# A decoder layer of two feed-forward steps, sparse attention and a pooling mixer on one core: gate and up of the first step by Strassen's seven products, and the mixers placed ahead in the program

## The chip, the core and the metric

The kernel runs on one core of one Trainium2 chip. The metric is device time in microseconds (us), the median of three runs. Five engines have their own instruction streams: PE (TensorE, the matrix products), DVE (VectorE), ACT (ScalarE), POOL (GpSimd) and SP (SyncE, which here only issues transfers). PEld is the loading of a stationary operand, which overlaps PE. PEclk is the granted TensorE clock as a share of its upper level.

## The reference

1024 tokens of width 1024 go through one layer, all in float32.

```
x = x + 0.5 * swiglu(rms_norm(x, ffn1_norm), ffn1_w_gate, ffn1_w_up, ffn1_w_down)   # inner width 2816
h = rms_norm(x, mix_norm)
q, k, v, qi, ki, wi, u = split(h @ w_in, (512, 512, 512, 256, 64, 4, 512))
q, k: RMS norm per head (8 heads x 64), rotary; qi (4 heads x 64), ki: rotary
I[t, s] = sum_h wi[t, h] * relu(qi[t, h] . ki[s])          # indexer, causal
attn = softmax over the 256 keys of highest I per query    # 8 heads
pooled = trailing means (2, 4, 8, 16) of u minus u, a 128x128 map per group, a scale
x = x + concat(attn, pooled) @ w_out
x = x + 0.5 * swiglu(rms_norm(x, ffn2_norm), ffn2_w_gate, ffn2_w_up, ffn2_w_down)
swiglu(x, g, u, d) = (silu(x @ g) * (x @ u)) @ d
```

## The kernel before

**Precision and units of work.** Each float32 operand is written as a high and a low part, and each product is three matrix multiplications (high by high, high by low, low by high; `mm3`, line 62). A full matmul has a 128x128 stationary operand and 512 moving columns. Weights come from DRAM as they are, 256 KB at a time, and are split on the chip by `weight`: ACT copies the high part (L171), DVE or POOL subtracts to get the low one (L172). Where `alone` is set DVE takes all of these, else POOL takes two of three.

**Halves.** The tokens are worked on in two halves of 512. A half's normalised and transposed activations live in the SBUF region XA (half 0) or XB (half 1). `ffn(h, ...)` goes over the 22 blocks of 128 inner columns: gate, up, silu times up (L200 to L204), and after each four blocks a down product that is added to x (L220). `mixer(h, ...)` holds index projection, indexer scores, pooling mixer, projections of v, k and q, top-k masks, attention and output projection. Its top-k (`top_masks`) finds each query's 256th highest score bit by bit in 31 steps; a step is an exclusive-or (L444), a count of one tile of 128 queries on ACT (L445) and of one on DVE (L429), a comparison (L450) and a conditional copy (L451), each waiting for the one ahead. `attention` goes over 4 head pairs, 2 query pairs and 2 heads, 16 turns; a turn has logits (L510, L511), softmax (L512 to L519), transposes (L533), splits (L537, L538) and value products (L541, tile `pv`), one turn behind the logits. Queries, keys, values and the mixer's output go through DRAM (`q_dr`, `k_dr`, `v_dr`, `m_dr`); the loads back are issued by POOL (L243, L488, L489, L497).

**What sets the order.** The kernel emits the work in the order of its last lines; a scheduler then orders each engine's instructions by what is ready in its model, earlier emitted work first, and by the free buffers of each tile pool (`BUFS`, `PBUFS`: 3 banks `fg` for the feed-forward steps; 2 `ba`, 2 `bt` and 1 `pv` for the mixers). Each engine runs its stream in that order. The emission is: x of half 0; the first step on half 0 (4 blocks); x of half 1, its norm; the rest of the first step on half 0; mixer 0 and the second norm of half 0; the whole first step on half 1; mixer 1 and the second norm of half 1; the second step on half 0, then on half 1. So `ffn(1, hT1, w1)`, 1584 full matmuls, stands beside mixer 0, and the second step of half 0 beside mixer 1, as what TensorE can do while a mixer waits; it is called filler below.

Of the kernel before, what the change touches and what calls it, by code (L numbers as in the profile page):

```python
# [18 lines left out]
S = 1024  # L19
# [13 lines left out]
HIGH = 10_000_000  # L33


@with_exitstack
def hybrid_layer(ctx: ExitStack, tc: tile.TileContext, x, ffn1_norm, ffn1_w_gate, ffn1_w_up,
# [7 lines left out]
    BUFS = {"r": 3, "w": 6, "a": 4, "t": 2, "br": 3, "bw": 3, "sc": 4, "mk": 4, "qm": 2,  # L45
            "st": 4, "cs": 1, "sel": 2, "x8": 4}
    PBUFS = {"fg": 3, "ba": 2, "bt": 2, "pv": 1}
    uid = [0]

    def t(tag, shape, dt=F32):  # L50
        uid[0] += 1
        return sb.tile(shape, dt, name=f"{tag}{uid[0]}", tag=tag, bufs=BUFS.get(tag, 1))
# [4 lines left out]

# [598 lines left out]
```

## Time and profile before

| what | value |
|---|---|
| median of 3 runs | 1988.79 us (1988.09 to 1989.29) |
| profiled execution, span from first to last instruction | 1985.0 us |
| PE busy in that span | 1936.2 us (98%) |
| DVE, ACT, POOL busy | 1115.9, 835.3, 555.2 us |
| mean granted TensorE clock | 0.995 |
| moved by DMA | 241.59 MB, mean 122 GB/s |

The span is that of one profiled execution; the median of the unprofiled runs is 3.8 us above it, which stands for what lies around the span. A share of busy time is an average over stages, and says nothing of what a stage waits for; that is read from windows of the trace.

### The profile page before, as it was taken

What the parts mean: (1) busy time and instruction counts of PE and PEld (TensorE: products, weight loads), DVE (VectorE), ACT (ScalarE), POOL (GpSimd) and SP (SyncE); (2) the same over time, 40 slices, a digit from 0 to 9 for tenths busy, and PEclk for the clock granted to TensorE, in tenths of its full rate; (3) what the DMA queues carried; (4) which work ended last, traced back from release to release, by engine and by line L of the source; (5) the groups of instructions that cost most, each with busy time, mean ns of one, the idle gap of its engine ahead of it and who ended that gap; (6) DMA issues with size and microseconds to landing.
All of it is one profiled execution on the core that took longest, in us unless ns stands there. A gap on an engine that the chain in (4) does not pass through costs nothing.

```text
span 1985.0 us, 25600 instructions
## 1 busy us (share of the span) xinstructions
PE 1936.2 (98%) x8904; PEld 1592.5 (80%) x8904; DVE 1115.9 (56%) x2242; ACT 835.3 (42%) x1550; POOL 555.2 (28%) x550
## 2 busy tenths in 40 slices
PE   7999999999999999999999998999999999999999
PEld 6888888888778888888888777678888878888887
DVE  5434433535985686242447999966767433444344
ACT  5323223344443566232443565437575332322231
POOL 2000000134448643344443343774332210000000
PEclk9999999999999999999999999999999999999999
DMA  7223323434365666333453225485653613333232
GB/s 210 88 89 101 96 90 97 137 110 128 100 167 154 174 157 198 130 91 97 135 137 97 78 93 149 136 199 128 131 140 113 201 42 96 102 95 96 91 106 90
DMA packets 304273, 241.59 MB, mean 122 GB/s; under 512 B 35472, under 2 KB 254736, under 8 KB 304144
## 3 DMA queue, kind: packets, MB, share of 16 engines
q1 hardware_dynamic: 285520, 207.45, 35.2%
q0 software_dynamic: 18624, 32.51, 7.6%
q8 instruction: 70, 1.15, 0.2%
q14 instruction: 59, 0.48, 0.1%
HBM read 208.45 MB, written 31.46 MB: 121 GB/s over the span
## 4 chain that ended last, share of the span: by engine, by line
PE 79%; DVE 13%; issue 3%; POOL 1%; ACT 1%; DMA 1%; SPq 0%; DVEq 0%; POOLq 0%; ACTq 0%
PE fg L62 63%; PE ba L62 6%; PE bt L62 5%; DVE x L429 4%; PE pv L62 2%; PE bt L533 2%; DVE sel L451 1%; DVE sel L450 1%; DVE sel L444 1%; DVE w L172 1%; DVE x L220 1%; POOL st L134 1%; PE ba L150 1%; DMA r<-in_ffn_w_gate_dram 0%; DVE sel L448 0%
## 5 line engine op out<-in xcount | busy, mean ns | idle before, releaser
L171 ACT CAST w<-r 128x512 fp32r<-128x512 f32 x528 | 325.5, 619 | 588.7 <-PE fg L62 304.0
L62 PE MATMUL fg<-XA,w 128*128 128x512 f32 x2112 | 519.6, 398 | 0.2
L62 PE MATMUL fg<-w,a 128*128 128x512 f32 x2112 | 505.4, 393 | 3.5 <-DVE x L220 2.3
L62 PE MATMUL fg<-XB,w 128*128 128x512 f32 x2112 | 497.5, 392 | 0.1
L62 PEld LDWEIGHTS fg<-XA,w 128*128 128x128 f32 x2112 | 394.8, 189 | 90.4 <-ACT XA L153 0.5
L62 PEld LDWEIGHTS fg<-w,a 128*128 128x128 f32 x2112 | 394.0, 188 | 87.5 <-DVE x L220 4.8
L62 PEld LDWEIGHTS fg<-XB,w 128*128 128x128 f32 x2112 | 395.4, 189 | 82.0 <-ACT XB L153 0.5
L172 DVE TENSOR_TENSOR w<-r,w 128x512 fp32r<-128x512 f32 x352 | 255.1, 727 | 317.0 <-ACT w L171 315.2
L172 POOL TENSOR_TENSOR w<-r,w 128x512 fp32r<-128x512 f32 x176 | 234.2, 1335 | 709.2 <-ACT w L171 357.0
L220 DVE SCALAR_TENSOR_TENSOR x<-fg,x 128x512 f32<-128x512 f32 x192 | 129.9, 686 | 122.0 <-PE fg L62 121.6
L172 POOL TENSOR_TENSOR bw<-br,bw 128x512 fp32r<-128x512 f32 (+1 forms) x75 | 95.1, 1273 | 154.8 <-ACT bw L171 146.8
L201 DVE TENSOR_TENSOR t<-t,fg 128x512 f32<-128x512 f32 x88 | 60.2, 684 | 106.4 <-PE fg L62 102.5
L171 ACT CAST bw<-br 128x512 fp32r<-128x512 f32 (+1 forms) x112 | 65.9, 596 | 119.9 <-PE bt L62 101.0
L200 ACT ACTIVATE t<-fg 128x512 f32<-128x512 f32 x88 | 52.4, 596 | 98.1 <-PE fg L62 97.7
L62 PE MATMUL ba<-bw,XB 128*128 128x512 f32 (+1 forms) x288 | 74.7, 384 | 7.1 <-DVE bw L172 2.7
L62 PE MATMUL ba<-bw,XA 128*128 128x512 f32 (+1 forms) x288 | 75.4, 386 | 2.1 <-ACT bw L171 2.1
L172 DVE TENSOR_TENSOR bw<-br,bw 128x512 fp32r<-128x512 f32 (+1 forms) x37 | 27.2, 736 | 86.8 <-ACT bw L171 86.4
L62 PE MATMUL bt<-bw,XB 128*128 128x512 f32 (+1 forms) x288 | 73.5, 382 | 1.6 <-ACT sc L365 1.3
L62 PE MATMUL bt<-bw,XA 128*128 128x512 f32 (+1 forms) x288 | 73.4, 382 | 0.2 <-DVE sel L448 0.2
L445 ACT ACTIVATE x<-sc,sel 128x384 bf16<-128x384 f32 (+1 forms) x62 | 44.6, 719 | 58.9 <-DVE sel L444 57.7
L204 POOL TENSOR_TENSOR a<-t,a 128x512 fp32r<-128x512 f32 x44 | 59.3, 1348 | 35.0 <-ACT a L203 34.6
L62 PEld LDWEIGHTS ba<-bw,XB 128*128 128x128 f32 x288 | 52.1, 189 | 20.2 <-DVE bw L172 3.9
(179 smaller groups left out, 1964.5 us busy)
## 6 DMA issues: line engine op xcount, KB each, us to landing
r<-in_ffn_w_gate_dram SPq DMA_DIRECT2D x176, 256.0 KB, 3.1
r<-in_ffn_w_up_dram SPq DMA_DIRECT2D x176, 256.0 KB, 3.0
r<-in_ffn_w_down_dram SPq DMA_DIRECT2D x176, 256.0 KB, 2.7
br<-in_w_in_dram SPq DMA_DIRECT2D x64, 256.0 KB, 2.7
br<-in_w_out_dram SPq DMA_DIRECT2D x32, 256.0 KB, 3.0
qm<-q_dr POOLq DMA_DIRECT2D x32, 256.0 KB, 4.1
x<-in_x_dram SPq DMA_DIRECT2D x8, 512.0 KB, 7.0
x_dr<-x SPq DMA_DIRECT2D x4, 1024.0 KB, 4.7
```

What stands on the lines that cost most here:

```text
L62: nc.tensor.matmul(o, lhs, rhs, start=start, stop=stop)
L134: nc.gpsimd.tensor_tensor(r[:, :n], r[:, :n], mhalf[:, :n], op=ALU.pow)
L150: nc.tensor.transpose(ps[:, i * 128:(i + 1) * 128], xn[i][:, k * 128:(k + 1) * 128], ident)
L171: nc.scalar.copy(w[:, 0, :n], raw[:, :n])
L172: eng.tensor_sub(w[:, 1, :n], raw[:, :n], f(w[:, 0, :n]))
L200: nc.scalar.activation(s, pg, AF.Silu)
L201: nc.vector.tensor_mul(s, s, pu)
L204: (nc.vector if alone[0] else nc.gpsimd).tensor_sub(a[:, 1], s, f(a[:, 0]))
L220: nc.vector.scalar_tensor_tensor(xo, ps, 0.5, xo, op0=ALU.mult, op1=ALU.add)
L429: nc.vector.tensor_scalar(masks[j][:, :ns[j]], sc[j][:, :ns[j]], thr, None, op0=op, op1=ALU.add, accum_out=cnt[:, j:j + 1])
L445: nc.scalar.activation(masks[0][:, :ns[0]], sc[0][:, :ns[0]], AF.Sign, bias=f(v1[:, 0:1]), accum_out=cnt[:, 0:1])
L533: nc.tensor.transpose(tp[:, j * 128:(j + 1) * 128], sm[ti][:, (2 * k2 + kk) * 128:(2 * k2 + kk + 1) * 128], ident)
```

## The change

**The first step.** Gate and up of all 1024 tokens are made by Strassen's scheme. The inputs are cut in two halves of tokens by two halves of the inner dimension, the weights in 2x2 blocks of 128 columns by 512 rows, and seven block products take the place of eight: 11 column pairs x 2 matrices x 7 products x 4 x 3 = 1848 matmuls for 2112. `norm_blocks` makes the seven input operands B once, from all 1024 tokens; `quad` loads 1 MB of weights, makes four sums on POOL and splits seven operands (ACT and DVE); `expand` adds the products up on DVE and writes the activations to DRAM (`a_dr`). `down(h)` reads them back, splits them and does the down products of one half.

**The mixers' weights.** `make_piece` loads each of 56 pieces during `expand`, splits it (ACT and POOL) and writes both parts to DRAM; `get_piece` reads 512 KB back, in both mixers, where 256 KB were loaded and split before.

**The order of emission.** `down(0)`, mixer 0, its second norm, `down(1)`, mixer 1, its second norm, second step of half 0, of half 1. What follows mixer 0 in emission and does not wait for it is `down(1)`, 528 matmuls.

**Inside the mixers.** Top-k takes all tiles of a half in one call (mixer 1: four, two counted on DVE and two on ACT) and replaces the conditional copy; the query and key rotary products and additions move largely from DVE to POOL; the split of the attention output moves to POOL and to the end of a head pair; q, k, v projections read PSUM once.

The diff, cut to its core:

```diff
+    def make_piece():
+        i, src = next(pieces, (None, None))
+        if src is None:
+            return
+        a, b = src.shape[1:]
+        raw = t("mk", [128, 512], role="praw")
+        nc.sync.dma_start(raw[:, :a * b].rearrange("p (a b) -> p a b", a=a), src)
+        part = [t("mk", [128, 512], F32R, "p") for _ in range(2)]
+        with tc.high_priority(offset=HIGH):
+            split(part[0][:, :a * b], part[1][:, :a * b], raw[:, :a * b], nc.gpsimd)
+        for l in range(2):
+            nc.sync.dma_start(p_dr[i][:, l, :a * b], f(part[l][:, :a * b]))
+    def get_piece(i, n=512):
+        w = t("bw", [128, 2, 512], F32R)
+        nc.sync.dma_start(f(w[:, :, :n]), p_dr[i][:, :, :n])
+        return w[:, :, :n]
...
+    def norm_blocks(which):
...
+        B = {p: (operand(p), operand(p)) for p in "1267543"}
+        homes = iter(["w"] * 5 + ["sc"] * 2 + ["qm"])
+        xn = {(h, i): normed(h, i, next(homes)) for h in range(2) for i in range(4)}
+        def turned(h, k):
+            ps = bank("ba" if h else "fg")
+            for i in range(4):
+                nc.tensor.transpose(ps[:, i * 128:(i + 1) * 128], xn[h, i][:, k * 128:(k + 1) * 128], ident)
+            return ps, gains[:, which, k:k + 1]
+        for k in range(4):
+            s = t("x8", [128, 4, 512])
+            b11, b22 = t("mk", [128, 512]), t("mk", [128, 512])
+            ps, g = turned(0, k)
+            nc.scalar.activation(b11, ps, AF.Copy, scale=g)
+            ps, g = turned(1, 4 + k)
+            nc.scalar.activation(b22, ps, AF.Copy, scale=g)
+            ps, g = turned(1, k)
+            nc.vector.scalar_tensor_tensor(s[:, 0], ps, g, b11, op0=ALU.mult, op1=ALU.subtract)
+            nc.vector.scalar_tensor_tensor(s[:, 1], ps, g, b22, op0=ALU.mult, op1=ALU.subtract)
+            nc.gpsimd.tensor_sub(s[:, 2], b22, s[:, 0])
+            ps, g = turned(0, 4 + k)
+            hi, lo = B["2"][0][k], B["2"][1][k]
+            nc.scalar.activation(hi, ps, AF.Copy, scale=g)
+            nc.vector.scalar_tensor_tensor(lo, ps, g, f(hi), op0=ALU.mult, op1=ALU.subtract)
+            nc.vector.scalar_tensor_tensor(s[:, 3], ps, g, s[:, 2], op0=ALU.mult, op1=ALU.subtract)
+            src = {"1": b11, "6": s[:, 2], "7": s[:, 1], "5": s[:, 0], "4": s[:, 3], "3": b22}
+            for p in "167543":
+                split(B[p][0][k], B[p][1][k], src[p], nc.vector if p in "165" else nc.gpsimd)
+        return B
...
+    def quad(W, j):
+        raw = t("x8", [128, NK, 256])
+        for k in range(0, NK, 4):
+            nc.sync.dma_start(raw[:, k:k + 4], rows(W, k, k + 4, 256 * j, 256 * j + 256))
+        s = t("x8", [128, 4, 4, 128])
+        a11, a12 = raw[:, 0:4, 0:128], raw[:, 4:8, 0:128]
+        a21, a22 = raw[:, 0:4, 128:256], raw[:, 4:8, 128:256]
+        src = {"1": a11, "6": s[:, 1], "7": s[:, 2], "5": s[:, 0], "2": a12, "4": a22, "3": s[:, 3]}
+        with tc.high_priority(offset=HIGH):
+            nc.gpsimd.tensor_add(s[:, 0], a21, a22)
+            nc.gpsimd.tensor_sub(s[:, 2], a21, a11)
+            nc.gpsimd.tensor_sub(s[:, 1], s[:, 0], a11)
+            nc.gpsimd.tensor_sub(s[:, 3], a12, s[:, 1])
+            out = {}
+            for p, tag in zip("1675243", ("w", "w", "qm", "w", "w", "qm", "w")):
+                out[p] = t(tag, [128, 2, 4, 128], F32R)
+                split(out[p][:, 0], out[p][:, 1], src[p], nc.vector)
+        return out
+    def product(o, w, b, first):
+        for k in range(4):
+            mm(o, w[:, 0, k], b[0][k], first and k == 0, False, not first)
+            mm(o, w[:, 0, k], b[1][k], False, False, not first)
+            mm(o, w[:, 1, k], b[0][k], False, k == 3, not first)
...
+    def expand(B, wg, wu, a_out, each=None):
+        nxt = quad(wg, 0)
+        todo = [(W, j) for j in range(NF // 2) for W in (wg, wu)][1:]
...
+                product(b1, w["1"], B["1"], True)
+                product(b6, w["6"], B["6"], True)
+                with tc.high_priority(offset=HIGH):
+                    nc.scalar.copy(u2, b1)
+                    nc.vector.tensor_add(u2, u2, b6)
+                b7 = bank(tags[2])
+                product(b7, w["7"], B["7"], True)
+                with tc.high_priority(offset=HIGH):
+                    nc.vector.tensor_add(u3, u2, b7)
+                b5 = bank(tags[3])
+                product(b5, w["5"], B["5"], True)
...
+                with tc.high_priority(offset=HIGH):
+                    nc.vector.tensor_add(u3, u3, b5)
+                    finish("22", u3)
+                product(b1, w["2"], B["2"], False)
+                with tc.high_priority(offset=HIGH):
+                    finish("11", b1)
...
+                nxt = quad(*todo.pop(0)) if todo else None
+                product(b5, w["3"], B["3"], False)
...
+            if each is not None:
+                for _ in range(6):
+                    each()
...
+    def down(h, a_in, wd):
+        for gr in GROUPS:
+            n = len(gr)
+            raw = t("XB", [128, 4, 512], role="rawa")
+            nc.sync.dma_start(raw[:, :n], a_in[gr[0]:gr[0] + n, :, h * HALF:(h + 1) * HALF].rearrange("k p c -> p k c"))
+            acts = []
+            for j in range(n):
+                a = t("a", [128, 2, 512], F32R)
+                split_shared(a[:, 0], a[:, 1], raw[:, j])
+                acts.append(a)
+            down_group(h, gr, acts, wd, 1.0)
...
     def qk_proj(h, hT, cs, which):
-        banks = proj(hT, (C_Q, C_K)[which], 512)
+        banks = proj(hT, P_QKV + 8 * which, 512)
         for i in range(4):
...
-            nc.vector.tensor_mul(n, ph, r[:, :, None].to_broadcast([128, NH, HD]))
-            m = t("mk", [128, 512]).rearrange("p (h d) -> p h d", d=HD)
+            nc.scalar.copy(s[:, 512:], banks[i])
+            nc.scalar.activation(s[:, :512], s[:, 512:], AF.Square)
...
+            r = rstd_of(ss, 8, HD)
+            nc.gpsimd.tensor_mul(n, n, r[:, :, None].to_broadcast([128, NH, HD]))
...
-            nc.vector.tensor_add(o, o, m)
-            pt = bank("pv")
+            nc.gpsimd.tensor_add(o, o, m)
...
         for bit in range(30, -1, -1):
-            nc.vector.tensor_scalar(v1, v, 1 << bit, None, op0=ALU.bitwise_xor)
-            nc.scalar.activation(masks[0][:, :ns[0]], sc[0][:, :ns[0]], AF.Sign, bias=f(v1[:, 0:1]),
-                                 accum_out=cnt[:, 0:1])
-            if m > 1:
-                nc.vector.tensor_scalar(th[:, 1:2], f(v1[:, 1:2]), -1.0, None, op0=ALU.mult)
-                count(1, ALU.is_ge, th[:, 1:2])
-            nc.vector.tensor_tensor(taken, cnt, goal, op=ALU.is_ge)
-            nc.vector.copy_predicated(v, taken, v1)
-        vf = v.bitcast(F32)
-        nc.vector.tensor_scalar(th, vf, -1.0, None, op0=ALU.mult)
-        nc.vector.tensor_max(mag, th, vf)
+            for j in range(d, m):
+                nc.scalar.activation(masks[j][:, :ns[j]], sc[j][:, :ns[j]], AF.Sign, bias=f(c[:, j:j + 1]),
+                                     accum_out=cnt[:, j:j + 1])
+            if bit:
+                nc.vector.tensor_scalar(cx, c, 1 << (bit - 1), None, op0=ALU.bitwise_xor)
+            for j in range(d):
+                count(j, ALU.is_ge, f(c[:, j:j + 1]))
+            nc.vector.tensor_tensor(taken, cnt, goal, op=ALU.is_lt)
+            nc.vector.scalar_tensor_tensor(c, taken, bit, cx if bit else c, op0=ALU.logical_shift_left,
+                                           op1=ALU.bitwise_xor)
+        nc.vector.tensor_scalar(th[:, act], f(c[:, act]), -1.0, None, op0=ALU.mult)
...
                         if last:
+                            parts = [t("mk", [128, HALF], F32R, "mo") for _ in range(2)]
+                            split(parts[0], parts[1], mo, nc.gpsimd)
                             for l in range(2):
-                                nc.sync.dma_start(m_dr[h][hp, :, l], f(mo[l]))
+                                nc.sync.dma_start(m_dr[h][hp, :, l], f(parts[l]))
...
+        top_masks(h, todo, [sc[i] for i in todo], [masks[i] for i in todo])
         attention(h, masks, region)
...
     load_x(0)
     load_gains()
-    hT0 = norm_transposed(0, 0, "A")
-    ffn(0, hT0, *w1, 0, 4)
     load_x(1)
     load_consts()
-    hT1 = norm_transposed(1, 0, "B")
-    ffn(0, hT0, *w1, 4, NF)
+    B = norm_blocks(0)
+    expand(B, ffn1_w_gate, ffn1_w_up, a_dr, make_piece)
+    load_x(0)
+    load_x(1)
+    alone[0] = True
+    down(0, a_dr, ffn1_w_down)
     alone[0] = False
     mixer(0, "A")
     hT0 = norm_transposed(0, 2, "A")
-    ffn(1, hT1, *w1, 0, NF)
+    down(1, a_dr, ffn1_w_down)
     mixer(1, "B")
     hT1 = norm_transposed(1, 2, "B")
-    ffn(0, hT0, *w2, 0, NF, out)
+    w2 = (ffn2_w_gate, ffn2_w_up, ffn2_w_down)
+    ffn(0, hT0, *w2, out)
     alone[0] = True
-    ffn(1, hT1, *w2, 0, NF, out)
+    ffn(1, hT1, *w2, out)
 def _consts():
```

**TensorE, attention of half 0.** Before, between a turn's logits (`ba`) and its transposes (`bt`, L533) and values (`pv`) stand products of the first step on half 1 (`fg`, operand XB, 512 columns each); these are rows of the kernel before:

```order
L62 MATMUL pv_4419<-XA_4291,XA_4293 128x256
L62 MATMUL fg_6636<-XB_661,w_6639 128x512
L62 MATMUL fg_6636<-XB_663,w_6639 128x512
L62 MATMUL ba_4509<-XA_4447,qm_4454 128x256 x2
L62 MATMUL ba_4519<-XA_4447,qm_4454 128x256 x2
L62 MATMUL pv_4419<-XA_4291,XA_4293 128x256 x7
L533 MATMUL bt_4478<-ident,sc_4400 128x128
L533 MATMUL bt_4478<-ident,sc_4410 128x128
L533 MATMUL bt_4478<-ident,sc_4400 128x128
```

These are rows of the changed kernel at the same place, the first turns behind the query transposes (`qt`); logits are `lg`, transposes `tp`:

```order
L519 MATMUL qt_5793<-ident,qk_5777 128x128 x4
L63 MATMUL lg_6034<-XA_6001,qm_6007 128x256 x2
L733 MATMUL tp_6045<-ident,p_6010 128x128
L733 MATMUL tp_6045<-ident,p_6011 128x128
L733 MATMUL tp_6045<-ident,p_6010 128x128
L733 MATMUL tp_6045<-ident,p_6011 128x128
L63 MATMUL pv_6044<-pt_6000,XA_6002 128x256
L63 MATMUL lg_6064<-XA_6001,qm_6058 128x512 x2
L63 MATMUL lg_6068<-XA_6001,qm_6058 128x512 x2
L63 MATMUL pv_6044<-pt_6000,XA_6002 128x256 x3
L63 MATMUL lg_6095<-XA_6001,qm_6058 128x512 x2
L733 MATMUL tp_6079<-ident,p_6027 128x128
```

No row of the first step stands between the query projection and the second step any more: the last product of `down(1)` is ahead of the end of the query projection (`pj`), and behind that follow 64 logits, 96 transposes, 96 value products, 192 output projections (`op`) and 32 norm transposes before the next `fg` row, which is the second step's first.

**GpSimd, the query rotary of half 0.** Before (`L324`, `L325` are the two rotary products, `L314` a table, `L172` and `L204` splits of the first step, `L497` loads the queries back):

```order
L172 TENSOR_TENSOR w_6428<-r_6426,w_6428 128x512
L172 TENSOR_TENSOR w_6463<-r_6461,w_6463 128x512
L324 TENSOR_TENSOR mk_4026<-sc_4016,st_4017 128x8x32
L325 TENSOR_TENSOR mk_4026<-sc_4016,st_4017 128x8x32
L172 TENSOR_TENSOR w_6487<-r_6485,w_6487 128x512
L314 TENSOR_TENSOR st_4043<-gqk,cs_2899 128x128
L497 DMA qm_4299<-q_dr_78 64x2x512 x2
L204 TENSOR_TENSOR a_6405<-t_6402,a_6405 128x512
L172 TENSOR_TENSOR w_6522<-r_6520,w_6522 128x512
```

Now (`L511` the normalising product, `L514`, `L515` and `L516` rotary products and addition, `L687` and `L688` loads of keys and values, `L696` that of the queries):

```order
L511 TENSOR_TENSOR qk_5696<-qk_5696,st_5703 128x512
L136 TENSOR_SCALAR st_5730<-st_5728 128x8
L514 TENSOR_TENSOR qm_5707<-qk_5696,st_5697 128x8x32
L515 TENSOR_TENSOR qm_5707<-qk_5696,st_5697 128x8x32
L137 TENSOR_TENSOR st_5730<-st_5730,mhalf 128x8
L687 DMA XA_6001<-k_dr 64x2x512
L688 DMA XA_6002<-v_dr 128x4x256
L687 DMA XA_6001<-k_dr 64x2x512
L516 TENSOR_TENSOR qk_5696<-qk_5696,qm_5707 128x512
```

```order
L511 TENSOR_TENSOR qk_5750<-qk_5750,st_5757 128x512
L514 TENSOR_TENSOR qm_5761<-qk_5750,st_5751 128x8x32
L515 TENSOR_TENSOR qm_5761<-qk_5750,st_5751 128x8x32
L136 TENSOR_SCALAR st_5784<-st_5782 128x8
L696 DMA qm_6007<-q_dr_78 64x2x512 x2
L516 TENSOR_TENSOR qk_5750<-qk_5750,qm_5761 128x512
L503 TENSOR_TENSOR st_5778<-gqk,mk_4747 128x128
L137 TENSOR_TENSOR st_5784<-st_5784,mhalf 128x8
L511 TENSOR_TENSOR qk_5777<-qk_5777,st_5784 128x512
```

Two operations of 512 columns per tile of queries were added to this engine, and the loads of the attention stand between them.

**The start.** Before, these are rows of TensorE: the last transposes of the first operands, and the first products (`fg`) among the next transposes:

```order
L150 MATMUL ba_135<-ident,sc_128 128x128
L150 MATMUL bt_142<-ident,sc_128 128x128
L150 MATMUL ba_149<-ident,sc_128 128x128
L150 MATMUL bt_156<-ident,sc_128 128x128
L62 MATMUL fg_191<-XA_103,w_194 128x512
L62 MATMUL fg_226<-XA_103,w_229 128x512
L150 MATMUL ba_163<-ident,sc_107 128x128
L150 MATMUL ba_163<-ident,sc_114 128x128
```

In the changed kernel the first product that needs a weight sum waits for `L263` on GpSimd, and these rows of GpSimd stand ahead of it (`L240` and `L166`, sums and splits of the inputs for all four k; `L261` to `L263`, the first weight sums):

```order
L166 TENSOR_TENSOR B_184<-x_297,B_182 128x512
L240 TENSOR_TENSOR x_383<-mk_385,x_383 128x512
L166 TENSOR_TENSOR B_177<-x_340,B_176 128x512
L262 TENSOR_TENSOR x_429<-x_426 128x512
L166 TENSOR_TENSOR B_185<-x_340,B_183 128x512
L261 TENSOR_TENSOR x_429<-x_426 128x512
L166 TENSOR_TENSOR B_177<-x_383,B_176 128x512
L166 TENSOR_TENSOR B_189<-mk_342,B_187 128x512
L166 TENSOR_TENSOR B_189<-mk_385,B_187 128x512
L166 TENSOR_TENSOR B_185<-x_383,B_183 128x512
L263 TENSOR_TENSOR x_429<-x_429,x_426 128x512
```

`L263` is the nineteenth operation of 512 columns on GpSimd; the first of them, `L240`, needs inputs of both halves.

## Rows read from the trace of the kernel before

**Rows 1.** Page, part 1: busy us, share of the span, instructions of each engine.
```profile
PE 1936.2 (98%) x8904; PEld 1592.5 (80%) x8904; DVE 1115.9 (56%) x2242; ACT 835.3 (42%) x1550; POOL 555.2 (28%) x550
```

**Rows 2.** Windows: stretch, us, busy us (instructions) by engine, PEclk, DMA share, GB/s.
```profile
0.00:23.31 23.31, 11.91 (x49) 8.92 (x49) 9.27 (x19) 11.72 (x19) 3.92 (x14) 1.00 0.78 233
484.00:570.00 86.00, 81.89 (x344) 65.01 (x343) 79.82 (x231) 45.08 (x111) 37.34 (x39) 0.98 0.45 131
660.00:790.00 130.00, 130.00 (x684) 110.34 (x683) 92.78 (x248) 87.49 (x181) 58.12 (x59) 1.00 0.68 173
1100.00:1350.00 250.00, 227.78 (x969) 178.93 (x968) 226.66 (x520) 128.91 (x249) 132.19 (x127) 0.98 0.50 134
1615.00:1620.00 5.00, 4.36 (x15) 3.17 (x16) 3.00 (x6) 2.43 (x4) 0.69 (x2) 0.50 0.01 3
1700.00:1950.00 250.00, 250.00 (x1105) 207.08 (x1104) 102.13 (x150) 73.03 (x121) 0.00 (x0) 1.00 0.32 96
```

**Rows 3.** Page, part 5, and lines by form: matmuls of one expansion and the weight splits.
```profile
L62 PE MATMUL fg<-XA,w 128*128 128x512 f32 x2112 | 519.6, 398 | 0.2
...
L171 ACT CAST w<-r 128x512 fp32r<-128x512 f32 x528 | 325.5, 619 | 588.7 <-PE fg L62 304.0 <-issue 145.1 <-DMA r<-in_ffn_w_up_dram 86.9
...
L172 DVE TENSOR_TENSOR w<-r,w 128x512 fp32r<-128x512 f32 x352 | 255.1, 727 | 317.0 <-ACT w L171 315.2
...
L172 POOL TENSOR_TENSOR w<-r,w 128x512 fp32r<-128x512 f32 x176 | 234.2, 1335 | 709.2 <-ACT w L171 357.0 <-DVE t L201 342.9 <-issue 8.9
```

**Rows 4.** Timeline of TensorE at the start: start us, us.
```profile
23.31 13.31 PE L62 MATMUL fg<-XA,w 128*128 128x512 f32 x56
```

**Rows 5.** Lines by form, the top-k steps of the first mixer's half and the second's.
```profile
L445 ACT ACTIVATE x<-x,sel 128x896 bf16<-128x896 f32 x31 | 32.4, 1044 | 57.9 <-DVE sel L444 56.7 <-DVE sel L451 1.2
...
L445 ACT ACTIVATION_READ_ACCUMULATOR x<-sc,sel 128x1 f32 x62 | 11.6, 187 | 0.0
...
L429 DVE TENSOR_SCALAR_CACHE_REDUCE x<-sc,sel 128x768 bf16<-128x768 f32 x33 | 33.3, 1008 | 0.3
...
L429 DVE TENSOR_SCALAR_CACHE_REDUCE x<-sc,sel 128x512 bf16<-128x512 f32 x33 | 24.6, 744 | 0.9
```

**Rows 6.** Line 451 in 480:580: duration min/median/max ns, first and last start us.
```profile
L451 DVE COPY_PREDICATED sel<-sel x31: 154/164/1229, 485.6 to 568.1; 128x2 int32<-128x2 int32 x31
```

**Rows 7.** Lines by form, GpSimd: pow, rope products.
```profile
L134 POOL TENSOR_TENSOR st<-st,mhalf 128x8 f32<-128x8 f32 x16 | 29.6, 1853 | 0.3
...
L324 POOL TENSOR_TENSOR mk<-sc,st 128x256 f32<-128x256 f32 x16 | 13.2, 826 | 0.3
```

**Rows 8.** Page, part 6: DMA issues: KB each, us to landing.
```profile
qm<-q_dr POOLq DMA_DIRECT2D x32, 256.0 KB, 4.1
...
q_dr<-mk SPq DMA_DIRECT2D x16, 256.0 KB, 3.2
...
m_dr<-mk SPq DMA_DIRECT2D x16, 256.0 KB, 6.0
...
XA<-m_dr POOLq DMA_DIRECT2D x4, 1024.0 KB, 8.1
```

**Rows 9.** Lines by form in 660:790, attention of the first half.
```profile
L538 DVE TENSOR_TENSOR XA<-bt,XA 128x512 fp32r<-128x512 f32 x24 | 16.3, 683 | 4.1 <-ACT XA L537 4.0
...
L511 DVE CUSTOM_DVE_ANT_0 sc<-ba,x 128x512 f32<-128x512 f32 x16 | 10.8, 686 | 1.8 <-PE bt L533 1.4 <-PE ba L62 0.2
...
L519 DVE TENSOR_SCALAR sc<-sc,st 128x512 f32<-128x512 f32 x16 | 9.2, 580 | 0.5
```

**Rows 10.** Line 511 and line 548 in 600:900.
```profile
L511 DVE CUSTOM_DVE_ANT_0 sc<-ba,x x32: 405/548/692, 669.7 to 768.0; 128x256 f32<-128x256 f32 x16, 128x512 f32<-128x512 f32 x16
...
L548 DVE TENSOR_TENSOR cs<-cs,pv x16: 391/419/425, 683.5 to 785.4; 64x256 f32<-64x256 f32 x16
```

**Rows 11.** Timeline of TensorE, last output projection to the next norm.
```profile
1608.82 1.07 PE L62 MATMUL bt<-bw,XB 128*128 128x512 f32 x4
...
1620.02 2.74 PE L62 MATMUL fg<-XB,w 128*128 128x512 f32 x9
```

More of the change, by code (lines that the diff above doesn't have):

```diff
@@ L89, in hybrid_layer @@
     x_dr = [dr.tile([HALF, D], F32, name=f"x_dr{h}") for h in range(2)]
+    a_dr = dr.tile([NF, 128, S], F32, name="a_dr")
+    p_dr = [dr.tile([128, 2, 512], F32, name=f"p_dr{i}") for i in range(NPIECE)]
     xs = [None, None]
@@ new lines, in hybrid_layer, with split_shared, down_weights @@
+    GROUPS = [range(k, min(k + 4, NF)) for k in range(0, NF, 4)]
+    alone = [True]
+    nsplit = [0]
+    def split_shared(hi, lo, src):
+        nsplit[0] += 1
+        with tc.high_priority(offset=HIGH):
+            split(hi, lo, src, nc.vector if alone[0] or nsplit[0] % 3 == 0 else nc.gpsimd)
+    def down_weights(wd, gr, c):
+        wts = []
+        for k in range(gr[0], gr[-1] + 1, 2):
+            raw = t("R", [128, 2, 512], role="rawd")
+            nc.sync.dma_start(raw, rows(wd, k, k + 2, c * 512, (c + 1) * 512))
+            for j in range(2):
+                w = t("w", [128, 2, 512], F32R, "wd")
+                split_shared(w[:, 0], w[:, 1], raw[:, j])
+                wts.append(w)
+        return wts
@@ new lines, in down_group @@
+    def down_group(h, gr, acts, wd, scale, done=None):
+        n = len(gr)
+        for c in range(2):
+            cols = slice(c * 512, (c + 1) * 512)
+            wts = down_weights(wd, gr, c)
+            for i in range(4):
+                ps = bank("fg", "dn")
+                tok = slice(i * 128, (i + 1) * 128)
+                for j in range(n):
+                    mm3(ps, acts[j][:, 0, tok], acts[j][:, 1, tok], wts[j][:, 0], wts[j][:, 1], j == 0, j == n - 1)
+                xo = x_at(h, i)[:, cols]
+                with tc.high_priority(offset=HIGH):
+                    if scale == 1.0:
+                        nc.vector.tensor_add(xo, ps, xo)
+                    else:
+                        nc.vector.scalar_tensor_tensor(xo, ps, scale, xo, op0=ALU.mult, op1=ALU.add)
+                if done is not None and gr[-1] == NF - 1:
+                    r0 = h * HALF + i * 128
+                    nc.sync.dma_start(done[0, r0:r0 + 128, cols], xo)
@@ L554, in attention @@
             ks, vt = load_kv(hp)
[L555 removed]
+            mo = t("mk", [128, HALF], role="o")
             for ql in range(2):
```

307 lines of the change are left out of this document (165 added, 142 removed).

## The prediction

> **What bounds the kernel now.** The page's busy shares come first: TensorE is busy 98% of the span, no other engine over 56% [rows 1]. A share is a mean over stages, so I read windows next. In 1700 to 1950, the second step alone, 1105 matmuls fill 250.00 us [rows 2]: 0.226 us each at the full clock, my price for every product below. Attention of half 0 lies in 660 to 790, and there too TensorE is busy 130.00 of 130.00 us [rows 2]: the first step's products of half 1 fill every wait. Time is lost in three places: the start, where a steady stream of products begins at 23.31 [rows 4]; top-k of half 0, 81.89 busy of 86.00; mixer 1, 227.78 busy of 250.00, so 22 [rows 2]. The kernel is thus bound by the count of matmuls plus some 45 us, as long as each mixer has filler beside it. The question is whether the new order still has.
>
> **The change part by part**, against the profiled execution's 1985.0 us; the median stands 3.8 above.
>
> *Seven products for eight.* 264 matmuls fewer at 0.226 us: **-60**. One of an expansion's products shows 519.6 / 2112 = 0.246 us busy [rows 3], and the change needs its sums in time, so -70 to -50. What makes the sums lies beside: a column pair is 168 matmuls, 38 us; POOL has 8 sums and 6 piece splits at 1.335 [rows 3], 18.7 us; DVE 14 splits at 0.727 [rows 3] and about 14 additions at some 0.686 (an eviction of that shape, by the reduction in [rows 9]), 20 us; the transfers, 2 MB of weights, 1 MB of activations and 4.5 MB of pieces, need 197 GB/s, and the start moves 233 [rows 2].
>
> This term was weighed against a rule. The second step's stream shows 0.226 us a matmul of 512 columns with its weight load [rows 2]. The Trainium skill, "TensorE: Matmul & The Clock Gate", section Back-to-back issue gap, gives about 131 ns for such a sustained stream. By it 264 fewer would save 35 us, and the whole sum would be 25 higher. The trace contradicts it here, so the trace decides.
>
> *Start.* Before, 16 products and 32 transposes (0.11 each at full clock) are done by 23.31 [rows 4]; that is 7.1 us of work, so 16 are lost. After, POOL's first sum needs both halves of x: 4.2 MB at 233 GB/s [rows 2] is 18 us, and square, power, product and transposes take about 4, so 22. Then 19 operations of 512 columns at 1.335 [rows 3] stand on POOL up to the first weight sum, 25 us, and its split on ACT and DVE 1.3 [rows 3]. The stream begins near 49, with one product (2.7 us) already done ahead, and 64 transposes (7 us) within: 39 lost. **+23**; at least +12 if half of POOL's queue runs before it matters, at most +35.
>
> A rule bears on that queue. Line 451, two columns on DVE, takes 154 ns at the least, 164 in the median and up to 1229 [rows 6]. The Trainium skill, "SBUF — State Buffer", section SBUF: two separate sides, says that a DVE operation with two SBUF inputs and a POOL operation that reads SBUF exclude each other, the later one standing still; the trace agrees with such a wait. By it, twelve DVE splits (8.7 us) would add to POOL's 25, 9 us more; that lies within the +35.
>
> *Entry to the down products.* The last product's additions, the write of `a_dr`, its load and split: about 3 + 3 + 1.3 us, of which the first groups' loads hide most: **+3** (0 to 5).
>
> *Top-k 0.* The order puts 211 matmuls, 47.5 us, beside its 31 steps. A step was 82.5 / 30 = 2.75 us [rows 6]. The new one has a DVE count (0.744 + 0.08 [rows 5]) and three small operations (0.16 to 0.36), some 1.6 us, with DVE's splits and evictions between, 17 us in all: 31 x 2.0 to 2.2 = 62 to 68. 47.5 of that is filled, and before lost 4: +10 to +16, I take **+12**. With no gain in the step it is +34, with all hidden 0.
>
> *Behind the query projection of half 0.* Here the order shows what moved: `down(1)`, 528 matmuls, is used up, and no product stands between the first logits and the second step. Three lengths follow one another.
> (1) Queries. Per tile POOL has table 0.57, power 1.85 [rows 7], scale 0.21, the new product 1.34, two rotary products 0.83 and 0.79, the new addition 1.34 (both as a 512-column operation, [rows 3]): 6.9 us. Two tiles make the first query pair: 13.8. Around them: read, square and sum on ACT and DVE 1.9, three attention loads issued by POOL ahead of the second tile 2.1, transposes and split 1.9, write 3.2, issue and load 5.3 [rows 8]. Sum 28.
> (2) Attention, 16 turns. DVE per turn: two masked reductions (0.41 or 0.686), two scalings 0.57, one or two splits 0.683 [rows 9], an addition 0.41 [rows 10], small ones: 3.6 or 4.9 us, together 68; the order puts 188 DVE rows there, 81 us by their forms. I take 80, since ACT and DVE pass each turn to and fro without cover.
> (3) The tail. Split 2, write of `m_dr` 6.0, load 8.1 [rows 8]: 16; then 24 output-projection matmuls 5.4 and the other 96, 21.7; then addition, square, power, product, transposes, split: before, 10 us from the last projection to a steady stream [rows 11], I take 9. Sum 52.
> 160 us, in which TensorE's own work is 32 (attention) + 43.4 (output projection) + 3.5 + 1.8 = 81; that it must do anyway: **+79**. Lower bound: 22 (half of the POOL chain overlapped) + 64 + 42 = 128, +47. Upper: 40 + 120 + 55 = 215, +134; 120 is what attention took before, 669.7 to 785.4 [rows 10], with other work on every engine.
>
> *Mixer 1.* Filler is the second step of half 0, as before. One top-k of four tiles: a step has two signs on ACT, 1.044 [rows 5] and by width 1.19, plus 2 x 0.187 to read, 2.6 us, and about 0.7 of comparison: 3.3 x 31 = 102, beside 377 matmuls (85 us): 17 lost. The second step's filler then ends about five turns ahead of the last: 10 to 15 lost, and 8 wait for the output. 38 against 22 before: **+15** (-10 to +40).
>
> Sum: -60 + 23 + 3 + 12 + 79 + 15 = +72. 1985.0 + 72 = 2057, with the 3.8, **2061 us**.
>
> **The rivals.**
> *A, the forecast*: attention 0 stands bare, 2061. For it: the order. Against: nothing in the order, only sizes.
> *B, not slower*: the bare stretch runs almost at TensorE's own pace. Place: query projection to second step. It decides when those 160 us shrink to 88 (81 + 7), because -60 + 23 + 3 + 12 + 15 = -7; with the stretch free the time is 1982. Against: DVE alone needs 64 to 81 in attention, and transfers and projections behind the last value 42.
> *C, the chain at its floor*: 128 us, +47, so 2029. For: before's turns shared DVE with splits and evictions, 92.78 busy of 130 [rows 2], which are gone.
> *D, attention no faster than before, at a low clock*: +134, 2116. For: TensorE's granted clock fell to 0.50 in 1615 to 1620 behind short transposes with waits [rows 2], and the bare stretch looks like that. Against: transposes and values are only a third of a turn.
> *E, the seven-product loop is fed too slowly*: 78 MB at 170 GB/s, attention's rate [rows 2], are 459 us for some 420: +40, 2101. Against: 233 GB/s at the start.
>
> **How the numbers follow.** A 0.50, C 0.18, D 0.16, E 0.08, B 0.08. A's own range is 2040 to 2085. The range 2014 to 2118 holds A, C, E and most of D, with the terms' bounds added by squares (start 12, top-k 14, stretch 45, mixer 25: about 54 each way). A measurement of this kernel tells 0.2%, 4 us, from no change. Faster comes from B alone, 0.05; B's rest, 0.02, is within 0.2%; slower, 0.93.
>
> **What would show it.** Right: TensorE nearly idle of products from the query projection to the second step, some 160 us at a third to half busy, PEclk low there; 1848 matmuls of the first step in 420 us; the stream's start near 49 us; top-k 1 with idle TensorE between steps. Wrong, if products stand in attention 0, or if a turn there takes under 4 us or over 7; if the first step is longer than 440 us; if the start is under 40.

## The result and the profile after

The changed kernel takes 2050.87 us (median of 4 runs, 2046.18 to 2051.53), the kernel before beside it 1988.70 (1988.09 to 1989.29): a ratio of 1.031, 95% interval 1.0295 to 1.0324. 2061 was forecast, 2014 to 2118 as its range. The profiled execution spans 2049.7 us, 64.7 more than before, where +72 was forecast.

Part 1 of the page of the changed kernel, which answers to [rows 1]:

```profile
PE 1913.4 (93%) x8640; PEld 1566.5 (76%) x8640; DVE 1146.2 (56%) x2038; ACT 800.6 (39%) x1490; POOL 648.9 (32%) x609
```

TensorE has 264 matmuls fewer, but it is busy 23 us less in a span 65 us longer. Its windows, with the columns of [rows 2]:

```profile
0.00:54.48 54.48, 21.03 (x77) 14.08 (x77) 36.80 (x48) 32.75 (x59) 38.86 (x42) 0.84 0.39 120
75.00:475.00 400.00, 400.00 (x1745) 327.48 (x1744) 240.90 (x288) 145.67 (x260) 181.96 (x132) 1.00 0.62 201
700.00:775.00 75.00, 69.15 (x294) 55.75 (x293) 69.47 (x211) 41.35 (x98) 34.90 (x35) 0.98 0.46 151
865.60:890.90 25.30, 3.38 (x13) 2.21 (x13) 6.06 (x9) 5.50 (x10) 24.34 (x28) 0.59 0.72 146
890.90:971.40 80.50, 60.35 (x296) 45.23 (x296) 61.04 (x188) 43.21 (x108) 23.16 (x32) 0.83 0.72 168
971.40:1026.30 54.90, 41.23 (x174) 32.34 (x173) 8.94 (x14) 8.31 (x16) 8.38 (x14) 0.89 0.55 188
1195.00:1300.00 105.00, 102.64 (x451) 84.26 (x450) 96.16 (x246) 85.59 (x159) 29.94 (x33) 1.00 0.57 177
1700.00:1950.00 250.00, 250.00 (x1104) 207.07 (x1104) 103.19 (x152) 74.71 (x124) 0.00 (x0) 1.00 0.32 97
```

The seven-product loop (75 to 475) runs full at a granted clock of 1.00, 201 GB/s beside it. The bare stretch is the fourth to sixth row: queries 25.3 us, attention 80.5, tail 54.9. In the second of them TensorE shows 60.35 us busy for work that fills 42 at the steady price: busy time taken alone would hide half of the loss.

So the account is made another way: the time up to a moment less the matmuls started by then, each at what it takes in a full stream (0.226 us for 512 columns as in [rows 2]; 0.152, 0.122 and 0.1085 for 324, 256 and 128, between starts in such streams). What is left is TensorE's lost time. By stage, in us (a stage's row is taken at its own ends):

```
stage                                        before   after   change
start, to 75                                   17.8    46.6    +28.8
first step, entry to down products             10.1    14.0     +3.9
top-k of half 0                                10.9    16.4     +5.5
waits within the query projection of half 0      -     11.9    +11.9
query projection to second step, half 0         4.5    79.6
  and the first 24 us behind it                         2.5    +77.6
mixer 1 and its second norm                    52.1    48.6     -3.5
end                                             5.4     5.9     +0.5
lost, all                                     100.8   225.5   +124.7
matmuls at the steady price                  1884.2  1824.5    -59.7
```

+124.7 - 59.7 = +65.0, the 64.7 of the spans within rounding. The -59.7 is a count times a price, 264 at 0.2262 us; what the trace adds is that the loop keeps that price nearly, 1745 matmuls in 400.00 us, 0.229 each. So the saving is there, and twice as much is lost elsewhere.

The start, timeline of TensorE, which answers to [rows 4]:

```profile
38.41 1.22 PE L63 MATMUL fg<-B,w 128*128 128x512 f32 x2 [2.66 <-ACT w L165]
46.42 4.63 PE L63 MATMUL fg<-B,w 128*128 128x512 f32 x10 [6.79 <-DVE w L166]
54.48 1.20 PE L63 MATMUL fg<-B,w 128*128 128x512 f32 x2 [3.42 <-ACT w L165]
55.48 4.09 PE L63 MATMUL fg<-B,qm 128*128 128x512 f32 x12
```

GpSimd and VectorE in that start, from their timelines:

```profile
39.55 1.26 POOL L166 TENSOR_TENSOR B<-x,B 128x512 fp32r<-128x512 f32 x1
40.77 1.71 POOL L262 TENSOR_TENSOR x<-x 128x512 f32<-128x512 f32 x1
...
50.84 1.71 POOL L166 TENSOR_TENSOR B<-x,B 128x512 fp32r<-128x512 f32 x1
52.51 1.26 POOL L263 TENSOR_TENSOR x<-x,x 128x512 f32<-128x512 f32 x1
```

```profile
39.02 0.74 DVE L239 SCALAR_TENSOR_TENSOR x<-ba,gains,mk 128x512 f32<-128x512 f32 x1
39.68 1.68 DVE L166 TENSOR_TENSOR B<-mk,B 128x512 fp32r<-128x512 f32 x1
```

The first sum of the inputs (`L240`) starts at 23.13, `L263` ends at 53.77: 30.6 us for 19 operations where 25 were forecast, 1.5 of them waits for inputs. A 512-column operation takes 1.26 or 1.71 us on GpSimd, and a split on VectorE 0.69 at its shortest and 1.68 here, while an operation with one operand in PSUM keeps its 0.74. The Trainium skill, "SBUF — State Buffer", section SBUF: two separate sides, has a VectorE operation with two SBUF inputs and a GpSimd operation take turns; the trace agrees in kind, and of the 9 us that the prediction worked out from the rule at most 5 came.

The bare stretch, timeline of TensorE from the end of the query projection:

```profile
848.53 7.96 PE L63 MATMUL pj<-bw,XA 128*128 128x512 f32 x24 [5.17 <-DMA bw<-p_dr]
...
875.52 1.11 PE L519 MATMUL qt<-ident,qk 128*128 128x128 f32 x4 [9.93 <-POOL qk L516]
880.26 1.12 PE L519 MATMUL qt<-ident,qk 128*128 128x128 f32 x4 [3.63 <-POOL qk L516]
888.72 1.12 PE L519 MATMUL qt<-ident,qk 128*128 128x128 f32 x4 [7.34 <-POOL qk L516]
890.87 1.19 PE L63 MATMUL lg<-XA,qm 128*128 128x256 f32 x4 [1.02 <-issue]
...
972.37 8.46 PE L63 MATMUL op<-bw,XA 128*128 128x512 f32 x36 [0.94 <-DMA bw<-p_dr]
989.42 29.48 PE L63 MATMUL op<-bw,XA 128*128 128x512 f32 x120 [8.59 <-DMA XA<-m_dr]
1020.61 0.33 PE L156 MATMUL ba<-ident,sc 128*128 128x128 f32 x1 [1.71 <-DVE sc L147]
```

Each wait names its releaser: GpSimd's rotary addition (L516) before the transposes, the round trip through `m_dr` before the last 120 output projections. Top-k: line 647 (the comparison of each step) for half 0, line 641 (the signs on ScalarE) for half 1: duration, first and last start; then the window of the steps of half 0.

```profile
L647 DVE TENSOR_TENSOR sel<-sel x31: 149/161/1257, 705.6 to 771.7; 128x2 int32<-128x2 f32 x31
L641 ACT ACTIVATE x<-x,sel x62: 1044/1096/1152, 1187.4 to 1292.2; 128x896 bf16<-128x896 f32 x31, 128x1024 bf16<-128x1024 f32 x31
705.60:771.70 66.10, 62.46 (x267) 50.53 (x265) 61.31 (x185) 38.35 (x92) 31.41 (x32) 0.97 0.45 146
```

Half 0: 31 steps in 66 us, within the 62 to 68 forecast, with 267 matmuls beside them where the order had shown 211. Half 1: 31 steps in 105 us, 3.4 each, with 451 (1195 to 1300 above) where it had shown 377.

### The profile page after: what moved, and what is told of

The parts are those of the page before. It is cut to its first block, busy times and chain, and to the rows that moved or that the text cites. A ratio compares the mean times of both kernels' runs of the same rounds, so it can differ in the third digit from the quotient of the medians.

```text
span 2049.7 us, 24399 instructions
## 1 busy us (share of the span) xinstructions
PE 1913.4 (93%) x8640; PEld 1566.5 (76%) x8640; DVE 1146.2 (56%) x2038; ACT 800.6 (39%) x1490; POOL 648.9 (32%) x609
## 4 chain that ended last, share of the span: by engine, by line
PE 72%; DVE 10%; ACT 5%; POOL 5%; issue 4%; DMA 3%; SPq 0%; POOLq 0%; ACTq 0%; DVEq 0%
PE fg L63 28%; PE dn L63 18%; PE bt L63 6%; PE ba L63 5%; PE pv L63 4%; PE pj L63 4%; PE op L63 3%; ACT x L641 2%; DVE x L622 2%; PE tp L733 1%; PE lg L63 1%; PE pu L63 1%; DVE sel L647 1%; DMA rawd<-in_ffn_w_down_dram 1%; POOL st L137 1%
## 5 line engine op out<-in xcount | busy, mean ns | idle before, releaser
L63 PE MATMUL dn<-wd,a 128*128 128x512 f32 x2112 | 510.1, 396 | 10.4 <-DVE x L367 4.5
L63 PEld LDWEIGHTS dn<-wd,a 128*128 128x128 f32 x2112 | 397.8, 190 | 98.5 <-DVE x L367 7.4
L63 PE MATMUL fg<-XA,w 128*128 128x512 f32 x1056 | 261.4, 395 | 0.1
L63 PE MATMUL fg<-XB,w 128*128 128x512 f32 x1056 | 243.0, 391 | 0.1
L63 PEld LDWEIGHTS fg<-XB,w 128*128 128x128 f32 x1056 | 199.1, 189 | 41.7 <-ACT XB L159 0.5
L63 PEld LDWEIGHTS fg<-XA,w 128*128 128x128 f32 x1056 | 196.9, 189 | 40.5 <-ACT XA L159 0.5
L165 ACT CAST w<-rawe 128x512 fp32r<-128x512 f32 x176 | 109.2, 622 | 211.0 <-PE fg L63 137.1
L166 DVE TENSOR_TENSOR w<-x,w 128x512 fp32r<-128x512 f32 x110 | 114.8, 1046 | 104.6 <-ACT w L165 104.1
L165 ACT CAST wd<-rawd 128x512 fp32r<-128x512 f32 x176 | 107.9, 621 | 156.5 <-PE dn L63 107.4
L166 DVE TENSOR_TENSOR w<-rawe,w 128x512 fp32r<-128x512 f32 x115 | 86.2, 754 | 99.8 <-ACT w L165 92.0
L166 DVE TENSOR_TENSOR wd<-rawd,wd 128x512 fp32r<-128x512 f32 x122 | 91.4, 756 | 67.0 <-ACT wd L165 64.0
L166 POOL TENSOR_TENSOR w<-rawe,w 128x512 fp32r<-128x512 f32 x61 | 80.0, 1316 | 146.0 <-ACT w L165 145.7
L166 POOL TENSOR_TENSOR p<-praw,p 128x512 fp32r<-128x512 f32 (+1 forms) x56 | 72.5, 1295 | 144.1 <-ACT p L165 144.1
L166 POOL TENSOR_TENSOR wd<-rawd,wd 128x512 fp32r<-128x512 f32 x54 | 74.6, 1387 | 116.8 <-ACT wd L165 116.6
L63 PE MATMUL fg<-B,w 128*128 128x512 f32 x396 | 97.4, 399 | 12.9 <-DVE w L166 6.8
```

The costliest lines, as they stand in the source:

```text
L63: nc.tensor.matmul(o, lhs, rhs, start=start, stop=stop, skip_group_check=goes_on)
L165: nc.scalar.copy(hi, src)
L166: eng.tensor_sub(lo, src, f(hi))
```

## The experiments

The theory: mixer 0 runs out of products, so attention, output projection and norm of half 0 stand bare, and with the later start that outweighs the seven products. Rivals: the mixers became slower in themselves (rotary on GpSimd, stored pieces, top-k), or the loss would be there whatever stands beside. Experiments 1, 2, 4, 7, 8 and 11 are one execution each; the four executions of experiment 5 lie 8 us apart. So small differences are read below from the lost time by stage, not from the times alone.

**1. Fewer products behind mixer 0, in the kernel before.**

```diff
+    ffn(1, hT1, *w1, 0, 14)
     alone[0] = False
     mixer(0, "A")
     hT0 = norm_transposed(0, 2, "A")
-    ffn(1, hT1, *w1, 0, NF)
+    ffn(1, hT1, *w1, 14, NF)
```

> The kernel before, with the first step of half 1 cut in two: its first 14 blocks are emitted ahead of mixer 0, and only the last 8 (576 matmuls, about the 528 of the changed kernel) behind it. No Strassen, no stored pieces, rotary and top-k as before. If the cause is that mixer 0 has too little filler, attention 0 stands bare here too and the time is 2055 to 2100 (1988.7 + 70 to 110). If the cause lies in what the change did inside the mixers or at the start, the place of these products costs little: 1988 to 2005.

2062.11 us, +74 to the runs beside it. Windows of top-k and projections, of attention 0 and of the tail in it:

```profile
730.00:875.00 145.00, 141.24 (x619) 114.16 (x618) 104.06 (x215) 56.43 (x116) 95.16 (x92) 0.99 0.57 154
878.00:957.00 79.00, 55.91 (x276) 41.13 (x276) 62.17 (x218) 49.58 (x124) 17.15 (x26) 0.85 0.69 172
957.00:1015.40 58.40, 44.80 (x184) 35.18 (x184) 11.85 (x19) 13.64 (x25) 17.64 (x20) 0.87 0.40 129
```

79 and 58 us, beside 80.5 and 54.9 of the changed kernel: none of the change is in this kernel but the few products left, and its attention and tail are as bare, with old rotary, old top-k and weights split in the mixer. Only the first part of the stretch, the queries, is covered here (the first row). Counted as lost time up to the second step's first product, this kernel has 98.1 us where the kernel before has 41.9, +56; another +19 lie in mixer 1, 70.9 for 51.8 between the second step's first products of the two halves.

**2. As 1, with more products left** (blocks 0 to 8 ahead, 8 to 22 behind).

> As the first experiment, but 14 blocks (1008 matmuls) of the first step of half 1 stay behind mixer 0 and 8 are emitted ahead. If the count of products left for mixer 0 is the cause, 432 more (98 us of TensorE work) take away most of the 73 us that 576 cost: 1995 to 2020, with the output projection of half 0 still bare. If it is the cut itself or the other order of emission, the time stays at 2050 to 2065.

2006.97 us. The same two stretches:

```profile
777.00:897.00 120.00, 118.42 (x620) 98.25 (x619) 92.40 (x243) 78.58 (x168) 46.78 (x48) 1.00 0.65 162
897.00:955.00 58.00, 58.00 (x252) 47.23 (x252) 15.43 (x23) 18.82 (x33) 22.61 (x23) 1.00 0.48 149
```

The whole time is +19 to the runs beside it, but mixer 0 has little part in that: up to the second step's first product 44.1 us are lost here, 41.9 in the kernel before and 98.1 in experiment 1. So in mixer 0 1584 and 1008 matmuls left cover nearly all, and 576 leave 56 us bare. It is the number of products left. The rest of the 19 is mixer 1, with 69.5 for 51.8, as in experiment 1; both kernels have it alike, so it is not the count behind mixer 0, and its cause was not looked for. Attention takes 120 us here, close to before [rows 10], and is covered; bare it takes 80, of which the changed kernel loses 39. The output projection was covered too, which was not expected.

**3. The changed kernel, its products held back**: 14 of 22 blocks of `down(1)` wait for the first sum of the query projection.

```diff
+            if h == 0 and which == 0 and i == 0:
+                nc.vector.tensor_copy(gate, ss[:, :1])
...
             raw = t("XB", [128, 4, 512], role="rawa")
+            if h == 1 and gr[0] >= 8:
+                nc.vector.tensor_copy(raw[:, 0, :1], gate)
```

> The changed kernel, with 14 of the 22 blocks of the second half's down product (336 matmuls, 76 us) held back until the query projection of half 0 has its first sum. If missing filler behind the query projection is the cause, these products fill that stretch and the time falls by 30 to 65 us, to 1985 to 2020; what keeps it from all 76 is that top-k 0 loses filler. If attention there is slow for a reason of its own (DVE and POOL as the bound), the products only lie elsewhere: 2040 to 2060.

2046.63 us (ratio to before 1.0297, 1.028 to 1.0314): 4 us less, within the interval of the changed kernel's own ratio. It lies in the second range, not the one that the theory had asked for. Windows of top-k and projections, then of attention:

```profile
675.00:825.00 150.00, 109.52 (x396) 82.51 (x396) 68.50 (x236) 47.26 (x108) 53.65 (x66) 0.82 0.59 174
825.00:925.00 100.00, 94.98 (x458) 78.17 (x458) 77.74 (x158) 48.04 (x107) 66.55 (x65) 0.96 0.67 165
```

In the changed kernel the same stretches are busy 142.09 of 150 and 58.47 of 100. The held products did fill the bare stretch, and left the one ahead of it bare instead: the number of the second range came, not its reason. My expectation took top-k and projections to feed TensorE by themselves; they don't.

**4. The changed kernel, `down(1)` emitted ahead of mixer 0.**

> The changed kernel with the second half's down product emitted ahead of mixer 0, so that nothing is left to fill mixer 0. If mixer 0 is short of products by their count, the 528 matmuls (119 us) that hid part of its waits are gone: 2110 to 2170. If they hid little (attention, where they do not stand, being all the loss), 2050 to 2075.

2061.21 us, in the second range, but it can't be read for it: the edit did not do what its expectation says. The order still put these products beside mixer 0, the last ending at 767 us in place of 836. So it tells only that the same 528 products, ending 70 us earlier, cost 10 more. With experiment 3: ending at 767, 836 and 935 us gives 2061, 2051 and 2047, and 178.5, 168.8 and 163.5 us lost up to the second step, with mixer 1 alike (48.6 to 48.7). Their place matters little; where mixer 0 without any would end was not measured.

**5. Rotary back on VectorE.**

```diff
-            nc.gpsimd.tensor_mul(n, n, r[:, :, None].to_broadcast([128, NH, HD]))
+            nc.vector.tensor_mul(n, ph, r[:, :, None].to_broadcast([128, NH, HD]))
...
-            nc.gpsimd.tensor_add(o, o, m)
+            nc.vector.tensor_add(o, o, m)
```

> The changed kernel with the normalising product and the last addition of the query and key rotary back on DVE, and the product read from PSUM. If the POOL chain is only the 28 us part of the bare stretch, it shortens by 4 POOL operations, some 5 us, and the time falls by 4 to 12 us, to 2039 to 2047. If the move to POOL is a main cause of the loss, it falls by 25 us or more.

2044.69 us (1.0276, 1.0259 to 1.0294): 6 less, as the small term says; the move to GpSimd is not a main cause of the loss.

**6. The last head pair's output kept on the chip.**

```diff
+                            if hp == 3:
+                                kept[h] = parts
...
-                m = mt[k // 2][:, k % 2]
+                m = [mt[k // 2][:, k % 2, l] for l in range(2)] if k != 3 else kept[h]
```

> The changed kernel, but the attention output of the last head pair of each half stays on the chip for the output projection, in place of a write to DRAM and a load. If the tail behind the last values of half 0 is bare as forecast, its 14 us of transfer go, less the turn from values to products: 8 to 14 us less, 2 to 6 of mixer 1 with it: 2031 to 2041. If the wait only passes to the weights' loads or the norm: 2046 to 2052.

2033.07 us (1.0226, 1.0212 to 1.024): 17.8 less. TensorE behind the last values of half 0:

```profile
983.50 2.88 PE L63 MATMUL op<-bw,mo 128*128 128x512 f32 x12
986.22 1.52 PE L63 MATMUL op<-bw,XA 128*128 128x512 f32 x6
987.92 18.15 PE L63 MATMUL op<-bw,XA 128*128 128x512 f32 x78 [0.18 <-DMA bw<-p_dr]
```

The wait of 8.59 is gone: the second step begins at 1016.2 in place of 1026.3, and another 7 us come in mixer 1, from the second step's first product to the last output projection. That is 10 of the 14 us that write and load were priced at [rows 8]: a round trip through DRAM that costs nothing under cover (experiment 12) costs most of its length in the open.

**7. Less work in the start**: the low parts of operands 7, 4 and 3 left out.

```diff
...
+            B[p] = (hi, hi if p in "743" else operand(p))
...
+                if p in "743":
+                    nc.scalar.copy(B[p][0][k], src[p])
...
```

> The changed kernel, with the low parts of three of the seven input operands left out (their high parts are read in their place, so the products are as many and the output is not the layer's). GpSimd then has 7 operations ahead of the first weight sum in place of 19. If the queue of sums and splits on GpSimd and VectorE sets the start, the stream begins 9 to 14 us earlier and the time is 2037 to 2043. If x, the transposes or ScalarE set it, 2048 to 2053.

2032.42 us, below either range. GpSimd's first weight sums are done early (its timeline; line 269 of this kernel is `L263` of the changed one):

```profile
37.34 1.72 POOL L267 TENSOR_TENSOR x<-x 128x512 f32<-128x512 f32 x1
39.14 1.60 POOL L269 TENSOR_TENSOR x<-x,x 128x512 f32<-128x512 f32 x1
```

TensorE's timeline there; the products from `qm`, which began at 55.48, begin at 48.91:

```profile
43.62 5.49 PE L63 MATMUL fg<-B,w 128*128 128x512 f32 x12 [3.76 <-DVE w L166]
48.91 3.28 PE L63 MATMUL fg<-B,qm 128*128 128x512 f32 x12
```

The sum is done at 40.7, 13 us earlier, but the lost time at 75 us is 39.3 for 46.6, 7 less: the next wait is for VectorE's split of the weights. The other 11 us of the gain lie behind 75 us, in an order that moved with it, and are not explained. So sparing GpSimd's queue gives back 7 of the 29, not all of it.

**8. Top-k in pairs again, in the changed kernel.**

> The changed kernel with top-k called for two tiles at a time, as before: in mixer 1 62 steps in place of 31. Mixer 1 was forecast to lose 15 and gained some 3. If the merged call is what shortened it, the chain is 31 steps of 2.5 to 2.8 us longer, some 80, against the same filler: 2085 to 2130. If top-k lies under the products anyway, 2050 to 2060.

2085.45 us, +35, at the lower end of the first range. Between the second step's first products of the two halves 81.8 us are lost, for 48.6: the merged call is worth that where products run out in mixer 1.

**9. The merged top-k in the kernel before.**

> The kernel before with the changed kernel's top-k alone: all tiles of a half in one call, no conditional copy. Putting the pairs back into the changed kernel cost 34 us. If that part of the change is worth as much here, mixer 1's 52 us of idle TensorE fall by 20 to 35 us: 1953 to 1970. If filler covers it in the kernel before, 1983 to 1990.

1984.71 us (0.9987, 0.9978 to 0.9996), 3 us less: the second range, in which products cover the top-k. In 1100 to 1350, beside [rows 2]:

```profile
1100.00:1350.00 250.00, 235.82 (x1022) 188.91 (x1021) 203.35 (x405) 147.02 (x269) 142.28 (x129) 0.99 0.53 139
```

TensorE idles 14 us there for 22; over the whole of mixer 1 the lost time falls by 5 (46.5 for 51.8), and 3 more are lost ahead of it.

**10 and 11. No stored pieces** (weights loaded and split in both mixers; the raw blocks in buffers shared with the rotary, then in two of the activations').

```diff
-        nc.sync.dma_start(f(w[:, :, :n]), p_dr[i][:, :, :n])
+        raw = t("mk", [128, 512], role="praw")
+        nc.sync.dma_start(raw[:, :a * b].rearrange("p (a b) -> p a b", a=a), src)
...
+            split(w[:, 0, :n], w[:, 1, :n], raw[:, :n], nc.vector if nsplit[0] % 3 == 0 else nc.gpsimd)
```

> The changed kernel without stored pieces: both mixers load 256 KB and split each weight again. If the stored pieces matter little, the waits for their loads (some 10 us on TensorE) go and splits come in: 2040 to 2060. If sparing VectorE, ScalarE and GpSimd the splits in the bare mixer was worth much, 2070 or more.

> The changed kernel without stored pieces again, with the raw weights in two buffers that mixer 0 does not use otherwise, in place of the six that the rotary products also use. If those shared buffers made most of the 96 us, the time is 2050 to 2090. If the splits in a bare mixer cost that by themselves (112 on ScalarE, VectorE and GpSimd), it stays above 2120.

2146.98 us (1.0801, 1.0783 to 1.0819), and 2193.57 us. Neither isolates the pieces. The second loses nothing in mixer 0, where its buffers are free (the second step begins at 1025.3 there, 1026.3 in the changed kernel): loading and splitting there cost no more than the stored pieces. It loses all in mixer 1, 193.5 us for 48.6. After 72 products no further one of the second step starts from 1050 to 1470, and mixer 1 runs without cover:

```profile
1050.00:1450.00 400.00, 276.33 (x1248) 210.69 (x1246) 282.97 (x670) 205.98 (x402) 133.16 (x151) 0.84 0.45 112
```

So it is a mixer without products once more, here a whole one, with the splits in it. That the products stayed away because their silu uses the same two buffers as the raw weights is argued, not shown; so is the part of the shared buffers in the first of the two, which loses 52 us up to the second step and 44 in mixer 1. What stored pieces are worth in mixer 1 stays open.

**12. A version from these**: the kernel before with merged top-k and the last head pair kept.

> The kernel before with the changed kernel's top-k and with the last head pair's output kept on the chip. By the bare places of mixer 1 (8 us at its output projection) 1975 to 1982; if products of the second step cover that wait too, as the ones of the first step did in mixer 0, 1983 to 1987.

1985.49 us, 0.9985 (0.9976 to 0.9994) of the kernel before: 3 us faster than it, at the edge of what can be told, and 65 less than the changed kernel. The top-k alone gave as much in experiment 9, so the kept pair, worth 18 us in the changed kernel, adds nothing that can be told here, where products cover the trip.

## Why the prediction was right

The sum was +72 and the spans differ by +65, by its own steps:
- **Seven products**, -60: 264 fewer at the steady price are 59.7, and the loop is bound by TensorE at 0.229 us a matmul. The 131 ns of the Trainium skill, "TensorE: Matmul & The Clock Gate", section Back-to-back issue gap, which the prediction weighed, were rightly set aside: no stream here shows them.
- **The bare stretch**, +79: lengths 25.3, 80.5 and 54.9 for 28, 80 and 52 forecast, TensorE's own work 81 in both, lost 79.6; the change in that row is +77.6. Experiments 1 and 2 show the cause: products left beside the mixer. One input was too high: 188 VectorE rows, put at 81 us by their forms, are busy 61.04 in that window. The length came out by the other reason given, that the engines pass each turn to and fro.
- **The start**, +23, is 28.8: the queue of 19 took 30.6 us for 25, most of it as GpSimd and VectorE took turns. In experiment 7, with 7 operations in that queue, the start still loses 39.3 of the 46.6, with TensorE waiting for VectorE's splits.
- **Not in the sum**: 11.9 us lost in the query projection, 5.2 of it for a stored piece's load. The forecast costed what replaces the split at nothing, and named no cover for its load.
- **Top-k 0**, +12, is 5.5, and **mixer 1**, +15, is -3.5. The failing step is the same: the 211 and the 377 matmuls beside the steps were counted in the order, which says what stands between two rows, not when they run. The steps took as long as forecast, 66 and 105 us, but 267 and 451 matmuls ran in that time. The tail of mixer 1 was right in kind: 24 us lost from 1575 to 1675 when the second step's products end.

The mechanism, the place and the size of the largest term are as forecast. That the whole came within 7 us is in part luck: the start and the query projection cost some 18 us more than the sum had, top-k 0 and mixer 1 some 25 less, and these nearly cancelled. In the chances, B's parts (0.05 and 0.02) make 0.07 of its 0.08.

Rival C's floor (47) and D's (134) were both off; the clock fell as D said, to a mean of 0.59 to 0.89 in the three windows, but attention took 80 us with it, not 120; how much of the 80 the low clock makes was not tried. E was wrong: 201 GB/s at full TensorE. The one part that fell is the idea that went with the forecast, that the place of the products would matter: experiments 3 and 4 moved them by 170 us for 14 us of time. It is their number that is short.

## What to carry to other kernels

A saving in work that must be done ahead of a latency-bound stage may spend the very work that covered this stage: price the cover as well as the saving, in matmuls left beside each stage. Here 264 matmuls (60 us) were saved, and the 1584 that stood beside mixer 0 became 528. Where cover is short, moving it moves the hole; shorten the bare chain instead, first where it goes through DRAM (18 us in experiment 6 for one round trip of each half).

## What the runs showed beyond that

Attention 0 takes 117 to 120 us under full cover and 79 to 80.5 bare: the products beside it lengthen it by half and cost next to nothing, since TensorE is busy 117.00 of 117 us meanwhile before, and 118.42 of 120 in experiment 2. A merged top-k was worth 35 us in one kernel and 3 in the other: the same edit has the price of its cover.
